# A PEER layer's first expert product: each expert column split in two pieces instead of three

## The chip, the cores and the metric

The kernel runs on one core of one Trainium2 chip. The metric is device time in microseconds of one execution, the median of several. Before the change it is 2997.09 us, the median of three runs that lay between 2996.09 and 2999.84 us. One further execution was taken with the hardware profiler; all rows below are from it.

## The reference

Two transformer blocks follow each other over 256 tokens of width 2048. The change lies in the last part of the second, a layer that chooses 16 experts for each of 8 heads out of 16384 and works on the rows that belong to them:

```python
def peer(xn, peer_w_q, peer_sub_keys, peer_u, peer_v):
    ...
    qh = (xt @ peer_w_q).reshape(T, PEER_HEADS, 2, PEER_HALF)
    sub = jnp.einsum("thpc,hpnc->thpn", qh, peer_sub_keys).astype(jnp.float32)
    v1, i1 = lax.top_k(sub[:, :, 0], PEER_TOPK)
    v2, i2 = lax.top_k(sub[:, :, 1], PEER_TOPK)
    ...
    experts = e1 * N_KEYS + e2
    gates = jax.nn.softmax(vals, axis=-1).astype(xn.dtype)
    def chunk_fn(args):
        xc, ec, gc = args
        u_sel = jnp.take(peer_u, ec, axis=0)
        h = jnp.einsum("cd,chkd->chk", xc, u_sel)
        a = jax.nn.gelu(h, approximate=False) * gc
        v_sel = jnp.take(peer_v, ec, axis=0)
        return jnp.einsum("chk,chkd->cd", a, v_sel)
```

`u` and `v` hold 16384 rows of 2048 numbers. The first expert product is `h`, the second the last line.

## The kernel before

The kernel is one long program. After the first block and the second block's convolution and attention comes the query product (`w_pq`), then the first expert product, then a choosing stage (lines 1169 to 1279), then the second expert product (lines 1315 to 1337).

The first expert product is computed in two ways at once. Of each row of `u`, the first 1408 numbers go through TensorE for **all** 16384 experts. The experts are ordered in 128 columns `e2` of 128 experts each, and one column is a block of 128 partitions by 1408 numbers, 11 chunks of 128. The other 640 numbers are fetched only for the chosen experts: GpSimd gathers 128 rows at a time with an indirect DMA (line 1026, 320 KB each, two per column, 256 in all), and VectorE multiplies each by the tokens and sums it (line 1040, a "dot" in what follows).

A column is handled in pieces (`UPC`), three of them before: 512, 512 and 384 numbers wide. For each piece SyncE issues a load into a raw buffer (line 421 or 424), ScalarE rounds it to `hi` (line 427), VectorE forms the remainder `lo` (line 428), and TensorE then does three matmuls for each chunk of 128 (`three`, lines 461, 464 and 465): `hi` with the tokens' high part, `hi` with their low part, `lo` with their high part. So the first two matmuls of a piece need `hi`, and the third needs `lo`. A column has 33 matmuls of 256 columns of tokens, the stage 4224.

The buffers are rings. `hi` and `lo` each have `UB[1]` buffers. Raw buffers come from two places (`u_raw`): `UB[0]` buffers of a pool, named `ur` in the trace, and `XRAW` slices of a block of the output array `ha` that isn't written yet, named `ha`. Before, that is 6 and 8 raw buffers. From column 92 on, the output array's block is about to be written, and pieces use the pool's buffers alone:

```python
        k = nraw[0] % (UB[0] + XRAW)
        if e2 >= (EB - 2) * EC - 4:
            k = 0
        nraw[0] += 1
        return None if k < UB[0] else xraws[k - UB[0]][:, :n]
```

A load into a raw buffer waits until the piece that was in it has both been rounded and had its remainder formed, which is the end of its line 428. The slices of `ha` lie where the query product's buffers and the first gathered rows (`kq`) lay, so they can be loaded only when the dots over `kq` are done.

Gathered rows have a ring of their own, 4 buffers and 6 more in the last block of `ha`. At column 106 (lines 1144 to 1146) all pending dots are done and the ring shrinks to 4. From column 1 on a gather waits for the last matmul of the column before it.

Each engine works its instructions off in one fixed order. That order is set when the program is built, by a scheduler that moves instructions among the stages, so pieces of the first columns are loaded and split while the query product still runs. A small generator, `step`, lets the steps of the heads' top-16 choice run on VectorE between the pieces until about column 100.

Of the kernel before, what the change touches and what calls it, by code (L numbers as in the profile page):

```python
# [30 lines left out]
NSUB = 1  # L31
STEPS = ((0, 0), (1, 0))
SEV = 5
UPC = ((0, 4), (4, 4), (8, 3))
EC = 16
EB = P // EC
XRAW, XROW = 8, 6
TK = (2, 4, 6)
EG = (0, 0, 0, 2, 4, 6, 8, 8)
TKU = (2, 12, 22, 32, 42)  # L40
UL = 126
UB = (6, 4)
VPACE, UPACE, UR = False, True, 4
N32 = (6, 7)
VR, VB, VLAG = 6, 3, 2
# [156 lines left out]
def body(ctx: ExitStack, tc: tile.TileContext, a, out):  # L202
# [214 lines left out]
    def wsplit(src, pool, n, nm, bufs, sb, size=None, raw=None):  # L417
        if first:
            raw = first.pop(0)
        elif raw is not None:  # L420
            nc.sync.dma_start(raw, src)
        else:
            raw = pool.tile([P, size or n], F32, tag="raw", name=nm + "r", bufs=bufs)[:, :n]
            nc.sync.dma_start(raw, src)
        hi = pool.tile([P, size or n], F32R, tag="hi", name=nm + "h", bufs=sb)[:, :n]
        lo = pool.tile([P, size or n], F32R, tag="lo", name=nm + "l", bufs=sb)[:, :n]
        S.activation(hi, raw, AF.Copy)  # L427
        low.append(V.tensor_tensor(lo, raw, hi.bitcast(F32), OP.subtract))  # L428
        return hi, lo
# [617 lines left out]
    def step():  # L1047
        while running:
            if next(running[0], True) is None:
                return True  # L1050
            running.pop(0)
# [53 lines left out]
    def block(b):  # L1105
        return ha[:, b].rearrange("p t b -> p (t b)")

    urows[0].more = [block(EB - 1)[:, k * (D - DU):(k + 1) * (D - DU)] for k in range(XROW)]
    xraws = [block(EB - 2)[:, k * UPC[0][1] * P:(k + 1) * UPC[0][1] * P] for k in range(XRAW)]
    nraw = [0]  # L1110

    def u_raw(e2, n):
# [7 lines that stand above are left out]
# [10 lines left out]
    for i in range(64):  # L1130
        ps = banks.one("ps_u")
        for b in range(2):
            e2 = 2 * i + b
            for p, (c0, n) in enumerate(UPC):
                if (b, p) in STEPS or (i % SEV == 0 and (b, p) == (1, 1)):
                    step()
                hi, lo = wsplit(a["u_dense"][e2][:, c0 * P:(c0 + n) * P], us, n * P, "u", *UB, UPC[0][1] * P,
                                u_raw(e2, n * P))
# [224 lines left out]
```

## Time and profile before

| | |
|---|---|
| median of three runs | 2997.09 us (2996.09 to 2999.84) |
| the profiled execution's own time | 2991.99 us |
| its span, first to last instruction | 2990.2 us |
| TensorE (PE) busy | 2923.6 us, 98% |
| VectorE (DVE) busy | 2395.6 us, 80% |
| ScalarE (ACT) busy | 1567.1 us, 52% |
| GpSimd (POOL) busy | 881.0 us, 29% |
| first expert product | from 1794.3 to about 2316.7 us of the span |

The profiled execution is 5.1 us under the median; 1.8 us of it lie outside the span. PE is TensorE's matmuls and PEld its weight loads. Matmuls overlap, so their durations add up to more than the time; what a matmul costs is read from how many start in a stretch. SPq is the queue of SyncE, which issues the loads.

### The profile page before, as it was taken

The numbers are of one execution on the slowest core, as the hardware profiler recorded it, in microseconds if no ns is written. First come the engines' busy times: TensorE is split into PE (matmuls) and PEld (weight loads), VectorE is DVE, ScalarE is ACT, GpSimd is POOL, SyncE is SP. The second block draws the span as 40 slices with busy tenths as digits, with TensorE's granted clock in tenths as the row PEclk, the third lists the DMA queues.
The fourth block names the chain that finished last, engine by engine and source line by source line (L and its number), as shares of the span: only waits on it lengthen the run. The fifth ranks groups of instructions, "written<-read, shape, count | busy, mean of one in ns | idle before, by whom it ended". The sixth has DMA issues, their size and how long they took to land. (4 is left out here: it accounts for less than half of the span.)

```text
span 2990.2 us, 49998 instructions
## 1 busy us (share of the span) xinstructions
PE 2923.6 (98%) x18472; PEld 2616.6 (88%) x18472; DVE 2395.6 (80%) x4392; ACT 1567.1 (52%) x2312; POOL 881.0 (29%) x670
## 2 busy tenths in 40 slices
PE   8999999999999999998999989999999999999999
PEld 7888888888888888888978989999999988888887
DVE  6567666777777776768998787999987988999998
ACT  5564555555545454546565534555555554444444
POOL 0000000000000000000000055666654897777786
PEclk9999999999999999999999999999999999999999
DMA  6545666656565666554534679999989348999998
GB/s 223 155 141 186 190 188 187 189 185 189 189 189 186 190 189 190 186 167 147 157 106 136 223 246 335 334 334 337 313 302 322 114 139 319 333 338 342 328 339 317
DMA packets 211143, 686.35 MB, mean 230 GB/s; under 512 B 29265, under 2 KB 47057, under 8 KB 210513
## 3 DMA queue, kind: packets, MB, share of 16 engines
q1 hardware_dynamic: 169776, 523.15, 53.4%
q0 software_dynamic: 41120, 160.01, 15.5%
q8 instruction: 144, 2.36, 0.3%
q14 instruction: 103, 0.84, 0.1%
HBM read 677.41 MB, written 5.64 MB: 228 GB/s over the span
## 5 line engine op out<-in xcount | busy, mean ns | idle before, releaser
L428 DVE TENSOR_TENSOR wl<-wr,wh 128x1024 fp32r<-128x1024 f32 x572 | 699.6, 1224 | 357.5 <-ACT wh L427 356.9
L427 ACT ACTIVATE wh<-wr 128x1024 fp32r<-128x1024 f32 x572 | 605.4, 1059 | 672.5 <-PE ps_dn L448 118.0
L976 POOL TENSOR_TENSOR tk_c<-tk_v 128x256 f32<-128x256 f32 x16 | 11.2, 702 | 1709.2 <-DVE tk_v L968 1708.9
L1026 POOL DMA_INDIRECT vrows<-in_v_rows,ex x256 | 393.8, 1538 | 119.3 <-DVE yg L1302 59.1
L465 PE MATMUL ps_u<-u_a,ul 128*128 128x256 f32 x1408 | 399.8, 284 | 9.7 <-DVE ul L428 9.5
L461 PE MATMUL ps_u<-u_a,uh 128*128 128x256 f32 x1408 | 397.9, 283 | 1.0 <-ACT uh L427 1.0
L464 PE MATMUL ps_u<-u_a,uh 128*128 128x256 f32 x1408 | 397.4, 282 | 0.0
L448 PE MATMUL ps_w_up<-u_a,wh 128*128 128x512 f32 x968 | 342.9, 393 | 0.0
L1318 ACT ACTIVATE vhi<-vraw 128x1472 fp32r<-128x1472 f32 x128 | 184.0, 1437 | 263.5 <-PE y L1335 260.9
L1334 PE MATMUL y<-vlo,ah 128*128 128x512 f32 (+1 forms) x768 | 297.8, 388 | 1.2 <-DVE vlo L1321 1.2
L1333 PE MATMUL y<-vhi,ah 128*128 128x512 f32 (+1 forms) x768 | 295.1, 384 | 3.5 <-ACT ah L1325 3.5
L1335 PE MATMUL y<-vhi,al 128*128 128x512 f32 (+1 forms) x768 | 296.5, 386 | 0.1
L465 PEld LDWEIGHTS ps_u<-u_a,ul 128*128 128x128 f32 x1408 | 266.4, 189 | 13.6 <-DVE ul L428 13.4
L450 PE MATMUL ps_w_up<-u_a,wl 128*128 128x256 f32 x968 | 270.4, 279 | 0.0
L461 PEld LDWEIGHTS ps_u<-u_a,uh 128*128 128x128 f32 x1408 | 266.5, 189 | 1.3 <-ACT uh L427 1.3
L464 PEld LDWEIGHTS ps_u<-u_a,uh 128*128 128x128 f32 x1408 | 266.4, 189 | 0.0
L448 PE MATMUL ps_dn<-ff,wh 128*128 128x512 f32 x704 | 248.7, 396 | 4.9 <-DVE ff L289 3.4
L1321 DVE TENSOR_TENSOR vlo<-vraw,vhi 128x1472 fp32r<-128x1472 f32 x128 | 216.1, 1688 | 40.1 <-ACT vhi L1318 40.0
L448 PEld LDWEIGHTS ps_w_up<-u_a,wh 128*128 128x128 f32 x968 | 181.4, 187 | 43.5
L1302 DVE SCALAR_TENSOR_TENSOR yg<-vrows,av,yg 128x576 f32<-128x576 f32 x256 | 208.6, 815 | 7.9 <-DMA vrows<-in_v_rows,ex 3.6
L427 ACT ACTIVATE uh<-ur 128x512 fp32r<-128x512 f32 (+1 forms) x228 | 135.6, 597 | 136.2 <-PE ps_u L464 97.7
L450 PE MATMUL ps_dn<-ff,wl 128*128 128x256 f32 x704 | 199.3, 283 | 3.8 <-DVE wl L428 3.8
(399 smaller groups left out, 7442.5 us busy)
## 6 DMA issues: line engine op xcount, KB each, us to landing
vraw<-in_v_dense SPq DMA_DIRECT2D x128, 736.0 KB, 7.2
wr<-in_w_up SPq DMA_DIRECT2D x176, 512.0 KB, 3.5
wr<-in_w_dn SPq DMA_DIRECT2D x88, 512.0 KB, 3.6
ur<-in_u_dense SPq DMA_DIRECT2D x152, 256.0 KB, 5.1
ha<-in_u_dense SPq DMA_DIRECT2D x104, 256.0 KB, 5.2
wr<-in_w_in SPq DMA_DIRECT2D x44, 512.0 KB, 3.5
wr<-in_w_cv SPq DMA_DIRECT2D x32, 512.0 KB, 3.6
wr<-in_w_ga SPq DMA_DIRECT2D x32, 512.0 KB, 3.5
```

Source lines behind the costliest of these rows:

```text
L427: S.activation(hi, raw, AF.Copy)
L428: low.append(V.tensor_tensor(lo, raw, hi.bitcast(F32), OP.subtract))
L448: PE.matmul(ps[:, j], hi[:, s], x[:, c0 + k, 0:2 * T], start=first and k == 0, stop=False, skip_group_check=True)
L450: PE.matmul(ps[:, j, T:], lo[:, s], x[:, c0 + k, 0:T], start=False, stop=last and k == KC - 1, skip_group_check=True)
L461: m = PE.matmul(o, wh, xh, start=start, stop=False, skip_group_check=True)
L464: PE.matmul(o, wh, xl, start=False, stop=False, skip_group_check=True)
L465: return PE.matmul(o, wl, xh, start=False, stop=stop, skip_group_check=True)
L1026: g = G.indirect_dma_start(out=v, out_offset=None, in_=a[name], in_offset=bass.IndirectOffsetOnAxis(ap=ex[:, tt, s:s + 1], axis=0))
L1321: vlo.append(V.tensor_tensor(lo, raw, hi.bitcast(F32), OP.subtract))
L1333: PE.matmul(o, st, hi[:, c:c + n], start=e2 == 0, stop=False, skip_group_check=True)
L1334: PE.matmul(o, st, lo[:, c:c + n], start=False, stop=False, skip_group_check=True)
L1335: mm = PE.matmul(o, sl, hi[:, c:c + n], start=False, stop=e2 == P - 1, skip_group_check=True)
```

## The change

Three tables of numbers change. A column is cut in two pieces of 768 and 640 numbers. The `hi` and `lo` rings have three buffers of 768 numbers each instead of four of 512. The raw ring has three pool buffers and five slices of `ha`, of 768 numbers, instead of six and eight of 512. For column 92 and after, that leaves three raw buffers.

```diff
-UPC = ((0, 4), (4, 4), (8, 3))
+UPC = ((0, 6), (6, 5))
 EC = 16
 EB = P // EC
-XRAW, XROW = 8, 6
+XRAW, XROW = 5, 6
...
-UB = (6, 4)
+UB = (3, 3)
```

TensorE's matmuls stay in the same order. The following places show what moves on the other engines; `x2` at the end of a row means twice in a row.

SyncE, from the last loads of the query product (`wr`) to the first loads into `ha`; `subd` and `sub` are scores that go out to memory and come back. Before:

```order
L424 DMA ur<-in_u_dense 128x512
L424 DMA ur<-in_u_dense 128x384
L424 DMA wr<-in_w_pq 128x1024 x4
L1080 DMA subd<-sub 128x512
L424 DMA wr<-in_w_pq 128x1024
L1080 DMA subd<-sub 128x512 x2
L421 DMA ha<-in_u_dense 128x512 x2
L421 DMA ha<-in_u_dense 128x384
```

Now:

```order
L424 DMA ur<-in_u_dense 128x768
L424 DMA wr<-in_w_pq 128x1024 x4
L1080 DMA subd<-sub 128x512
L424 DMA wr<-in_w_pq 128x1024
L1080 DMA subd<-sub 128x512 x2
L421 DMA ha<-in_u_dense 128x640
L421 DMA ha<-in_u_dense 128x768
```

The first piece that needs a slice of `ha` was the seventh, the first of column 2; it is now the fourth, the second of column 1.

VectorE, where the query product ends and the expert product begins; `kq,hg` are dots, `ul<-ur,uh` and `ul<-ha,uh` the remainders of pieces. Before:

```order
L1040 ISA kq,hg<-kq,xg 128x640
L1040 ISA hg 128x1
L428 TENSOR_TENSOR ul<-ur,uh 128x512
L428 TENSOR_TENSOR ul<-ur,uh 128x384
L428 TENSOR_TENSOR ul<-ha,uh 128x512 x2
```

Now:

```order
L1040 ISA kq,hg<-kq,xg 128x640
L1040 ISA hg 128x1
L428 TENSOR_TENSOR ul<-ha,uh 128x640
L428 TENSOR_TENSOR ul<-ha,uh 128x768
L428 TENSOR_TENSOR ul<-ha,uh 128x640
```

Before, the fifth and sixth pieces' remainders (the last two pieces of column 1) stand behind the last of the dots over `kq`. Now the remainders of all three pieces that have pool buffers stand earlier, among the query product's, and the first one behind the dots is that of a piece in `ha`.

VectorE late in the stage, where only the pool's buffers are used, one column's work. Before:

```order
L428 TENSOR_TENSOR ul<-ur,uh 128x512 x2
L428 TENSOR_TENSOR ul<-ur,uh 128x384
L1040 ISA urows,hg<-urows,xg 128x640
L1040 ISA hg 128x1
L1040 ISA urows,hg<-urows,xg 128x640
```

Now:

```order
L428 TENSOR_TENSOR ul<-ur,uh 128x768
L428 TENSOR_TENSOR ul<-ur,uh 128x640
L1040 ISA urows,hg<-urows,xg 128x640
L1040 ISA hg 128x1
L1040 ISA urows,hg<-urows,xg 128x640
```

The dots keep their place behind a column's pieces; a column has one remainder less.

## Rows read from the trace of the kernel before

**Rows 1.** The page's first part and its line of TensorE's granted clock.

```profile
PE 2923.6 (98%) x18472; PEld 2616.6 (88%) x18472; DVE 2395.6 (80%) x4392; ACT 1567.1 (52%) x2312; POOL 881.0 (29%) x670
...
PEclk9999999999999999999999999999999999999999
```

**Rows 2.** Busy time in stretches of the first expert product; the first row names the columns.

```profile
core 0: us, PE busy (x) PEld busy (x) DVE busy (x) ACT busy (x) POOL busy (x), PEclk, DMA share, GB/s
...
2000.00:2100.00 100.00, 99.59 (x835) 98.99 (x834) 95.80 (x250) 56.39 (x93) 63.39 (x51) 1.00 0.97 338
...
2245.30:2308.80 63.50, 63.14 (x531) 62.78 (x529) 50.29 (x105) 34.96 (x56) 32.94 (x28) 1.00 0.96 337
```

**Rows 3.** Waits of TensorE, 1815 to 2220 us: in total, times, longest, us.

```profile
PE ps_u L465 <- DVE ul L428: 2.8, 7, 0.5
```

**Rows 4.** Waits from 2165 to 2317 us, all engines.

```profile
ACT uh L427 <- DMA ur<-in_u_dense: 17.2, 15, 1.9
...
PE ps_u L465 <- DVE ul L428: 3.9, 6, 2.2
```

**Rows 5.** Waits of SyncE's queue, 2165 to 2317 us.

```profile
SPq L424 <- DVE ul L428: 85.3, 71, 6.6
```

**Rows 6.** A piece's load, rounding and remainder, timelines of SyncE, ScalarE and VectorE.

```profile
2256.36 0.33 SPq L424 DMA_DIRECT2D ur<-in_u_dense  x1
...
2262.43 0.63 ACT L427 ACTIVATE uh<-ur 128x512 fp32r<-128x512 f32 x1 [1.92 <-DMA ur<-in_u_dense]
...
2264.16 0.82 DVE L1040 CUSTOM_DVE_ANT_0 urows<-urows,xg 128x640 f32<-128x640 f32 x1 [1.88 <-DMA urows<-in_u_rows,ex]
2264.91 0.08 DVE L1040 DVE_READ_ACCUMULATOR2_ANT hg<- 128x1 f32 x1
2264.91 1.76 DVE L428 TENSOR_TENSOR ul<-ur,uh 128x512 fp32r<-128x512 f32 x3
```

**Rows 7.** Landing times of pieces issued from 2250 to 2317 us.

```profile
DMA to landing us min/median/max: 3.5/5.1/6.3
```

**Rows 8.** Landing times of the two pieces issued at 2238.5 and 2238.9 us.

```profile
DMA to landing us min/median/max: 2.5/2.5/2.5
```

**Rows 9.** Landing times of gathered rows issued from 2250 to 2317 us.

```profile
DMA to landing us min/median/max: 4.7/5.8/7.0
```

**Rows 10.** Groups by shape, 2250 to 2317 us: count, busy us, mean ns, idle before.

```profile
L428 DVE TENSOR_TENSOR ul<-ur,uh 128x512 fp32r<-128x512 f32 x32 | 21.1, 686 | 4.4 <-ACT uh L427 3.4 <-PE ps_u L465 0.7
L427 ACT ACTIVATE uh<-ur 128x512 fp32r<-128x512 f32 x32 | 20.3, 634 | 19.2 <-PE ps_u L464 8.1 <-DMA ur<-in_u_dense 7.9 <-DVE ul L428 3.2
...
L428 DVE TENSOR_TENSOR ul<-ur,uh 128x384 fp32r<-128x384 f32 x16 | 8.8, 553 | 1.6 <-ACT uh L427 1.4
L427 ACT ACTIVATE uh<-ur 128x384 fp32r<-128x384 f32 x16 | 8.4, 525 | 8.9 <-PE ps_u L464 8.8
```

**Rows 11.** TensorE's matmuls of the product in the stage's first 6.75 us.

```profile
1794.30:1801.05 6.75, 5.79 (x47) 5.67 (x47) 0.00 (x0) 1.00 0.79 226
```

**Rows 12.** The stage's beginning, timelines of TensorE, VectorE, SyncE and ScalarE.

```profile
1804.43 0.58 PE L465 MATMUL ps_u<-u_a,ul 128*128 128x256 f32 x1 [3.18 <-DVE ul L428]
...
1803.69 1.15 DVE L428 TENSOR_TENSOR ul<-ur,uh 128x512 fp32r<-128x512 f32 x2
...
1803.90 4.66 SPq L421 DMA_DIRECT2D ha<-in_u_dense x8
...
1808.70 0.63 ACT L427 ACTIVATE uh<-ha 128x512 fp32r<-128x512 f32 x1 [9.73 <-DMA ha<-in_u_dense]
...
1810.11 0.39 PE L465 MATMUL ps_u<-u_a,ul 128*128 128x256 f32 x1 [0.23 <-DVE ul L428]
```

**Rows 13.** Two-microsecond stretches at the beginning, columns as in rows 2.

```profile
1806.00:1808.00 2.00, 2.00 (x12) 2.00 (x11) 0.00 (x0) 0.00 (x0) 0.00 (x0) 0.57 0.90 299
```

**Rows 14.** VectorE at column 106, first and last of nine dots, and what follows.

```profile
2223.84 0.82 DVE L1040 CUSTOM_DVE_ANT_0 urows<-urows,xg 128x640 f32<-128x640 f32 x1
...
2229.81 0.82 DVE L1040 CUSTOM_DVE_ANT_0 urows<-urows,xg 128x640 f32<-128x640 f32 x1
...
2230.55 1.75 DVE L428 TENSOR_TENSOR ul<-ur,uh 128x512 fp32r<-128x512 f32 x3
```

**Rows 15.** Stretches behind column 106, columns as in rows 2.

```profile
2232.00:2236.00 4.00, 4.00 (x27) 4.00 (x27) 0.91 (x2) 1.15 (x2) 1.42 (x2) 0.70 0.84 284
2236.00:2240.00 4.00, 3.53 (x30) 3.32 (x29) 2.62 (x5) 2.17 (x4) 1.12 (x1) 1.00 0.59 203
2240.00:2244.00 4.00, 3.74 (x31) 3.54 (x30) 4.00 (x12) 1.67 (x3) 2.65 (x3) 1.00 0.84 241
```

## Prediction

> **What bounds the kernel now.** I read the page's first part, then the stage's busy time by stretches, then who waits for whom, then single timelines. TensorE is busy 98% of the span at a granted clock that reads full in every slice [rows 1], so time is won or lost only where TensorE waits. Inside the stage it hardly does: from 1815 to 2220 us it waited 2.8 us in all, each time for a piece's remainder on VectorE [rows 3], and from 2165 to the end 3.9 us [rows 4]. Its pace undisturbed is 531 matmuls in 63.50 us [rows 2], 0.1196 us each; a column of 33 takes 3.95 us. The reader should see how thin the cover over this is. VectorE is busy 95.8 of 100 us in the middle and 50.3 of 63.5 us near the end, and the DMA engines run at a share of 0.96 to 0.97 in both [rows 2]. In the last part, where only the pool's raw buffers are used, SyncE's queue waits for remainders 71 times, 85.3 us in all [rows 5], and ScalarE waits 15 times for a load [rows 4]. A ring in which the load waits for the buffer and the next engine waits for the load is already turning there at nearly the rate TensorE needs.
>
> **The change part by part.**
>
> *Fewer, larger splits.* From 686 and 553 ns for 512 and 384 numbers [rows 10] a remainder costs about 1.04 ns a number on top of a fixed part, so 768 and 640 take 952 and 819 ns; a column's remainders fall from 1.925 to 1.771 us, 0.15 us less, 20 us of VectorE over 128 columns. Roundings by the same rows take 852 and 743 ns. TensorE hides all of that: it waits for remainders 2.8 us in 405 [rows 3], which is the most that faster splits can return there. Against it stands that `hi` and `lo` of a piece now may be begun two pieces ahead of TensorE (11 chunks, 3.95 us) and take 1.7 us, where it was three pieces (11 to 12 chunks) and 1.3 us, so 0.4 us of lead is lost beside dots that block VectorE for 0.8 us each [rows 14]. I take 0 for columns 2 to 91, with bounds of -2.8 (all waits gone) and +5 (they grow almost threefold).
>
> The Trainium skill, Perfetto Trace Analysis, section Optimizing Scalar/DVE Operations, says that larger operations improve throughput if the engine is saturated, and that where Scalar or Vector aren't saturated but cause bubbles on other engines, breaking instructions up lets work finish sooner. By its first half the middle of the stage would gain, by its second the end would lose; the 95.8% and 79% agree with a reading in both directions.
>
> *The start.* Before, TensorE did 47 matmuls [rows 11], then stood 3.18 us, because the fifth piece's remainder is behind the dots over `kq`; it then ran the 66 matmuls of six pieces out and took the seventh piece's third matmul, the first that needs its remainder, at 1810.11 [rows 12]. Now three pieces, 17 chunks or 51 matmuls, are all split early, so it stops 4 matmuls later, near 1801.6. The fourth piece is in `ha`, whose first load was issued at 1803.90 and reached ScalarE at 1808.70 [rows 12]. With a quarter more bytes (0.15 us), a rounding of 0.74 and a remainder of 0.82 us, its third matmul starts at about 1810.5, 0.4 us later than the 1810.11 and with 15 matmuls fewer done: 0.4 + 15 x 0.1196 = 2.2 us lost. Behind its wait TensorE ran at a clock of 0.57 [rows 13], the lower level, for 14 or so matmuls; I expect that spell once again, so no difference. Bounds: 0.5 (the dots come sooner) and 5 (two slow spells).
>
> *The ring of three.* From column 92 on a load waits for the piece three before it, not six. One turn is: release to issue 0.05, landing, landing to rounding 0.11, rounding 0.80 (mean of 852 and 743), 0.03, then the remainder's place in VectorE's queue, and the remainder 0.885 (mean of 952 and 819). A turn of the old ring [rows 6]: issued 2256.36, rounded from 2262.43, the remainder held until 2264.91 by a dot that itself waited for its row. Without landing and queue that is 1.87 us. For the queue I take 0.5 us, a third of the 1.5 us that two dots in the way hold it, at 0.75 us from dot to dot [rows 14]. Three pieces give TensorE 16.5 chunks, 49.5 matmuls, 5.92 us of work. So the turn fits if landing takes up to 3.55 us.
>
> Landing is what the trace doesn't show for this ring. Under load the smaller pieces take 5.1 us at the median [rows 7]. Two pieces of 256 and 192 KB issued when VectorE had just held everything up took 2.5 us [rows 8], and gathered rows of 320 KB, the size of the new smaller piece, take 5.8 us [rows 9]. So the ends are 2.5 and 5.8 us. With at most three own pieces in flight the queue in front is shorter, but the gathers stay and each piece has half as many bytes again; I take 4.4 us, nearer to rows 7. Then a turn is 4.4 + 1.87 + 0.5 = 6.77 us against 5.92, 0.85 us lost each. Pieces 187 to 255 make 23 turns: 19.6 us. The first turn starts with some 0.9 us of lead, so **18.7 us**. At 2.5 us nothing is lost (turn 4.87 us); at 5.8 us a turn is 8.17 us, 23 x 2.25 = 52 us.
>
> The waits would be short, one of some 0.3 us before each piece. Two such waits behind column 106 left the granted clock at 1.00 (second and third row of [rows 15]), so I add nothing for the clock.
>
> The Trainium skill, DMA: Bandwidth & Descriptors, section Anatomy of one DMA — SWDGE (gpsimd) path, fits a DMA's time as 2.0 us plus bytes over 436 GB/s. For 384 and 320 KB that is 2.9 and 2.75 us, an estimate by that page; the turn would be 5.2 us and nothing would be lost, which speaks against my sum. The page's fit (2.5 to 2.6 us for 192 to 256 KB) agrees with the 2.5 us of the idle moment and not with the 5.1 us under load.
>
> *The drain at column 106.* Nine dots in a row, 2223.84 to 2230.55, hold back the remainders [rows 14], and TensorE lost a wait of 2.2 us [rows 4] and a slow spell at 0.70 [rows 15]. With a starved ring there is less lead before it, but the three loads land meanwhile. I take +1, bounds -2 and +4.
>
> Sum: 0 + 2.2 + 18.7 + 1 = 21.9, so 22 us; the profiled execution's 2991.99 us would become 3014. The median of the runs is 5.1 us above that execution, so **3019 us**.
>
> **The rivals.**
>
> *The ring of three keeps up* (same). Condition: landing at or below 3.55 us, because fewer bytes are queued. For it: rows 8. Against it: DMA share 0.96 [rows 2] and the two gathers per column, whose amount doesn't change. Left are 2.2 us at the start and 1 at the drain: 3000 us.
>
> *VectorE's relief shows* (faster). Place: the whole stage. With one remainder less a column and landing below 3.55 us, waits of 2.8 and 3.9 us go [rows 3, 4], and with the drain's wait its slow spell (27 matmuls in 4 us where 33.4 fit [rows 15], 0.8 us); if the start also costs nothing, 2997 - 7.5 = 2989.5 us. It decides only if both the landing and the start go well. Against it: the lead that is lost.
>
> *Landing as slow as the gathers'* (much slower). For it: same size, same engines, 5.8 us at the median [rows 9]. Against it: a starved ring asks for less. 52 + 3 = 55: 3052 us.
>
> **How the numbers follow.** Forecast 0.65, keeping up 0.12, relief 0.09, slow landing 0.14. The forecast's own range is 3009 to 3031 us: landings of 4.0 and 4.9 us give turns of 6.37 and 7.27 us, 9.5 and 30 us with the lead taken off, and 3 us beside. A measurement here can tell about 0.2%, 6 us, from no change. Forecast and slow landing lie above 3003 us, together 0.79; keeping up lies within, a little of it beyond: same 0.12; faster 0.09. The range takes in the upper edge of keeping up and most of the way to slow landing, 2998 to 3044.
>
> **What the changed profile would show.** Right: from column 92 on SyncE's waits for remainders stay, ScalarE's waits for `ur` grow from 17.2 us and 15 times to dozens of waits, TensorE waits for roundings and remainders some 20 us between column 92 and the end, the clock stays at 1.00 there, and loads land in 4.0 to 4.9 us. At the start one wait of about 8 us in place of 3.18 and 0.96. From column 3 to 91 nothing changes. Wrong: landing at 3.5 us or less, or TensorE's waits spread over the columns before 92, or a clock of about 0.5 between the short waits, which would cost far more.

## The result and the profile after

The changed kernel takes 3014.84 us, the median of four runs (3011.78 to 3018.78), against 2996.59 us for the kernel before on the same chip (four runs, 2995.85 to 2999.84). The ratio is 1.0063, 95% interval 1.0050 to 1.0077: slower, by 15 to 23 us. The forecast was 3019 us, 22 us more than before. The profiled execution took 3015.2 us with a span of 3013.4 us, 23.2 us longer than the span before. The profiled execution of before lay 4.6 us under the median of these runs and this one lies 0.4 us above its own, so 5 of the 23 us are a matter of which execution was profiled.

Where the 23.2 us lie is read off TensorE's timeline, by the start of the first matmul of a column (the last number of a row is what the stretch that ends there grew by):

| us of the span | before | after | grew by |
|---|---|---|---|
| query product begins | 1680.23 | 1681.31 | 1.1 |
| column 0 begins | 1794.37 | 1798.56 | 3.1 |
| column 3 begins | 1814.29 | 1819.12 | 0.6 |
| column 92 begins | 2167.63 | 2173.67 | 1.2 |
| column 104 begins | 2215.78 | 2226.72 | 4.9 |
| column 108 begins | 2236.22 | 2249.69 | 2.5 |
| last matmul of column 127 begins | 2316.51 | 2338.36 | 8.4 |
| end | 2990.22 | 3013.41 | 1.3 |

So 15.8 us of the growth are in columns 92 to 127 (the tail in what follows), where only the pool's three raw buffers serve, and 3.8 us in the query product and the first three columns together. The query product and the first columns belong together, since the first load into `ha` is issued when the gathered rows over `kq` are done, whatever TensorE has reached: 123.7 us behind the query product's begin before, 123.3 us now.

The busy time by stretches, columns as in [rows 2], for columns 92 to 127 of the kernel before and then of the changed one:

```profile
2167.63:2316.51 148.88, 145.03 (x1195) 143.42 (x1194) 124.78 (x276) 78.59 (x130) 76.35 (x63) 0.99 0.91 311
```

```profile
2000.00:2100.00 100.00, 99.19 (x829) 98.78 (x828) 95.29 (x224) 52.71 (x67) 64.09 (x53) 1.00 0.95 333
...
2173.67:2338.36 164.69, 152.75 (x1195) 146.72 (x1194) 121.52 (x240) 73.69 (x95) 74.79 (x64) 0.98 0.85 286
```

The same 1195 instructions of TensorE (36 columns of 33 matmuls and seven others) take 148.9 us in one and 164.7 us in the other. VectorE, ScalarE and the DMA engines do less per microsecond, not more: nothing got saturated; rather, the engines wait for each other in a circle. In the middle (first row of after) nothing has changed against [rows 2].

The waits in columns 92 to 127 of the changed kernel (in total, times, longest, us), with [rows 4, 5] as their counterpart:

```profile
ACT uh L427 <- DMA ur<-in_u_dense: 75.1, 50, 6.5
DVE ul L428 <- ACT uh L427: 39.4, 37, 4.1
...
PEld ps_u L465 <- DVE ul L428: 13.5, 24, 2.1
PE ps_u L465 <- DVE ul L428: 8.0, 17, 1.8
...
PE ps_u L461 <- ACT uh L427: 3.4, 4, 1.6
```

```profile
SPq L424 <- DVE ul L428: 104.0, 66, 5.7
```

ScalarE's waits for a load went from 15 (17.2 us) to 50 (75.1 us), for 69 pieces. From there the wait is passed on: VectorE waits for the rounding, TensorE for either. The last line is SyncE's queue, which still waits for remainders before it issues a load, as it did before [rows 5]. TensorE's waits are 11.4 us here and not the 22.5 us that it takes beyond its undisturbed 142.2 us (36 columns of 3.95 us): the view counts a wait from the modelled end of the matmul before it, and leaves out what a lower clock costs. One piece of that ring, in the timelines of ScalarE, VectorE and TensorE (start, duration, instruction, idle time before it and its releaser):

```profile
2289.76 0.85 ACT L427 ACTIVATE uh<-ur 128x768 fp32r<-128x768 f32 x1 [1.19 <-DMA ur<-in_u_dense]
2295.22 0.74 ACT L427 ACTIVATE uh<-ur 128x640 fp32r<-128x640 f32 x1 [4.61 <-DMA ur<-in_u_dense]
...
2295.99 0.82 DVE L428 TENSOR_TENSOR ul<-ur,uh 128x640 fp32r<-128x640 f32 x1 [4.15 <-ACT uh L427]
...
2296.01 0.39 PE L461 MATMUL ps_u<-u_a,uh 128*128 128x256 f32 x1 [1.59 <-ACT uh L427]
2296.23 0.28 PE L464 MATMUL ps_u<-u_a,uh 128*128 128x256 f32 x1
2296.87 0.39 PE L465 MATMUL ps_u<-u_a,ul 128*128 128x256 f32 x1 [0.36 <-DVE ul L428]
```

All three engines stand until the load of this piece lands at 2295.11; it was issued at 2288.31, when the piece three before it had its remainder. It is one of the slowest: it and the two behind it took 6.8, 7.8 and 7.5 us to land. Landing times of the pieces in this stretch, which before were [rows 7]:

```profile
DMA to landing us min/median/max: 2.8/4.5/7.8
```

Two stretches of the changed kernel behind its longest waits show TensorE at a lower granted clock (the seventh number, behind the five engines' busy times; 0.50 is the lower of its two levels, and 0.64 a mean over both):

```profile
2246.00:2249.00 3.00, 3.00 (x16) 3.00 (x15) 0.18 (x1) 0.00 (x0) 0.13 (x1) 0.50 0.84 296
...
2296.00:2300.00 4.00, 3.63 (x17) 3.43 (x18) 3.25 (x6) 2.34 (x3) 1.29 (x1) 0.64 0.57 189
```

The first answers to the spell that the kernel before also had behind its drain [rows 15]. The second is new and had not been forecast: 18 matmuls started 0.21 us apart in place of 0.12, 1.7 us.

### The profile page after: what moved, and what is told of

It is laid out like the page before. It is cut to its first block, busy times and chain, and to the rows that moved or that the text cites. A ratio compares the mean times of both kernels' runs of the same rounds, so it can differ in the third digit from the quotient of the medians.

```text
span 3013.4 us, 49238 instructions
## 1 busy us (share of the span) xinstructions
PE 2935.5 (97%) x18472; PEld 2625.6 (87%) x18472; DVE 2391.7 (79%) x4264; ACT 1551.9 (51%) x2184; POOL 872.0 (29%) x670
## 4 chain that ended last, share of the span: by engine, by line
PE 75%; DVE 7%; POOL 6%; issue 5%; DMA 4%; ACT 2%; DVEq 0%; POOLq 0%; ACTq 0%; SPq 0%
PE ps_w_up L448 11%; PE ps_w_up L450 6%; PE ps_dn L448 5%; POOL vrows L1026 5%; PE ps_u L465 4%; PE ps_u L464 4%; PE ps_u L461 4%; PE ps_dn L450 3%; PE y L1335 2%; PE y L1334 2%; PE y L1333 2%; DMA ur<-in_u_dense 2%; PE ps_w_ga L448 2%; PE ps_w_cv L448 2%; PE ps_w_gb L448 2%
## 5 line engine op out<-in xcount | busy, mean ns | idle before, releaser
L1026 POOL DMA_INDIRECT vrows<-in_v_rows,ex x256 | 385.4, 1505 | 130.2 <-DVE yg L1302 70.0
L465 PEld LDWEIGHTS ps_u<-u_a,ul 128*128 128x128 f32 x1408 | 268.5, 191 | 17.8 <-DVE ul L428 17.6
L427 ACT ACTIVATE uh<-ur 128x768 fp32r<-128x768 f32 (+1 forms) x141 | 112.9, 802 | 167.7 <-DMA ur<-in_u_dense 77.1
```

What stands on the lines that cost most here:

```text
L465: return PE.matmul(o, wl, xh, start=False, stop=stop, skip_group_check=True)
L1026: g = G.indirect_dma_start(out=v, out_offset=None, in_=a[name], in_offset=bass.IndirectOffsetOnAxis(ap=ex[:, tt, s:s + 1], axis=0))
```

## The experiments

The theory was the prediction's: from column 92 a piece's load waits for the piece three before it, and issue, landing, rounding and remainder (the turn) take longer than TensorE needs for three pieces. The rivals are the larger pieces themselves, or the shorter `hi` and `lo` rings, or VectorE's dots, or something of the last part (the drain, the block written there).

**One raw buffer more.** `four_raw` keeps the two pieces and gives the pool four raw buffers, two of each size:

```diff
-UB = (3, 3)
+UB = (4, 3)
...
-raw = pool.tile([P, size or n], F32, tag="raw", name=nm + "r", bufs=bufs)[:, :n]
+raw = (pool.tile([P, n], F32, tag="raw%d" % n, name=nm + "r", bufs=2) if nm == "u" else
+       pool.tile([P, size or n], F32, tag="raw", name=nm + "r", bufs=bufs)[:, :n])
```

> The changed kernel with four pool raw buffers instead of three (two of 768 and two of 640 numbers, which fit; the hi and lo rings stay at three of 768). Theory A, the ring of loads: a turn (issue, landing, rounding, remainder; 6.9 us in the changed kernel's last part) now has four pieces of TensorE work, 7.9 us, so it fits; columns 92 to 127 take 148 to 151 us instead of 164.7, and the time falls to 2998 to 3003 us. Rival B, the larger pieces and the hi and lo ring of three: both are unchanged, so the time stays at 3011 to 3018 us and the last part at 160 us or more.

Ratio to before 1.0024 (1.0014 to 1.0034), 3001.73 us. Columns 92 to 127 of this kernel, columns of the row as above:

```profile
2173.91:2325.09 151.18, 145.44 (x1195) 143.50 (x1194) 122.37 (x240) 73.32 (x95) 74.55 (x64) 0.99 0.89 306
```

151.2 us against 164.7 with three and 148.9 before: one more buffer returns 13.5 of the 15.8 us, with the piece size, the dots and the shorter `hi` and `lo` rings left as they were. (The tail is 0.2 us over the expected range.) The time in front of column 3 did not come back: here SyncE issues the pool's first loads only from 1799.5 us on, behind the scores that it sends to memory, where the changed kernel issues the first at 1703.8; why they stand there in its order isn't shown.

**The old pieces in a short ring.** `thirds4` and `thirds5` are the kernel before with `UB = (4, 4)` and `UB = (5, 4)` in place of `(6, 4)`.

> The kernel before, with its pieces of 512, 512 and 384 numbers and four hi and lo buffers, but four pool raw buffers instead of six. Theory A: a turn is about 4.4 us landing plus 1.45 us of own work plus 0.4 us of queue, 6.3 us, against four pieces or 5.3 us of TensorE work; 26 turns lose 1.0 us each, less the 6 us that this part had lost anyway: 3012 to 3025 us, and ScalarE waits for loads in most pieces after column 92. Rival B: pieces are small and the hi and lo ring has four, so nothing is lost: 2995 to 3000 us.

> The kernel before with five pool buffers in the raw ring from column 92 on. By the ring's sum five pieces of 4,4,3 chunks give TensorE 18.3 chunks, 6.6 us of work, and a turn with landing 4.8, 1.57 us of its own work (roundings and remainders of 512 and 384 numbers) and 0.5 us of queue is 6.9 us: 0.3 us short per turn of five pieces, 22 turns, 6 us. So columns 92 to 127 take 150 to 157 us, ratio 1.000 to 1.003, between the kernel before (six, 148.9) and four (171.9). Rival, a threshold in bytes in flight or in the number of loads rather than a turn: five behaves as four, over 162 us and over 1.005.

`thirds4` took 3020.51 us, 1.0080 (1.0064 to 1.0097), `thirds5` 3001.50 us, 1.0025 (1.0016 to 1.0035). Columns 92 to 127 of the first, then of the second:

```profile
2173.83:2345.72 171.89, 154.92 (x1195) 146.86 (x1194) 123.89 (x276) 79.80 (x130) 72.02 (x63) 0.98 0.84 270
```

```profile
2170.30:2326.21 155.91, 148.00 (x1195) 145.06 (x1194) 124.62 (x276) 78.59 (x130) 72.14 (x63) 0.98 0.88 299
```

With unchanged piece sizes the tail takes 148.9, 155.9 and 171.9 us for six, five and four buffers: the loss comes with the ring's length and not with the size of a piece. Five buffers lie between six and four, as a turn has it; a threshold would have put them with four. The turn's parts, as means over the pieces behind column 92 (from the timelines; the turn also holds the 0.03 to 0.04 us from release to issue; "need" is the matmuls of a ring's pieces times TensorE's 0.1196 us; `no_dots` and `no_gather` follow below):

| us | landing | to rounding | rounding | queue on VectorE | remainder | turn | need |
|---|---|---|---|---|---|---|---|
| before, six | 5.09 | 0.81 | 0.60 | 1.08 | 0.65 | 8.28 | 7.89 |
| `thirds5` | 4.91 | 0.27 | 0.60 | 0.83 | 0.65 | 7.28 | 6.58 |
| `thirds4` | 4.39 | 0.16 | 0.59 | 0.62 | 0.65 | 6.45 | 5.26 |
| after, three larger | 4.62 | 0.15 | 0.79 | 0.47 | 0.89 | 6.94 | 5.92 |
| `four_raw` | 5.17 | 0.56 | 0.79 | 1.03 | 0.89 | 8.48 | 7.89 |
| `no_dots` | 4.69 | 0.33 | 0.79 | 0.07 | 0.89 | 6.81 | 5.92 |
| `no_gather` | 3.32 | 0.54 | 0.79 | 0.64 | 0.89 | 6.20 | 5.92 |

A measured turn is the pace of the whole ring, so what it has above the need is the loss itself and no reason for it: "to rounding" and "queue" hold waiting that others cause. Landing, rounding and remainder alone hold none. Their sum lies above the need in the three kernels with the slowest tails (6.30 us of 5.92 after, 5.63 of 5.26 in `thirds4`, 6.37 of 5.92 in `no_dots`) and under it in the others (6.34 of 7.89 before, 6.85 of 7.89 in `four_raw`, 5.00 of 5.92 in `no_gather`). `thirds5` is the nearest, 6.16 of 6.58: the 0.4 us that are left don't cover its queue of 0.83 us.

**No gathers.** `no_gather` is the changed kernel without gathers from column 92 on (`late[0]`); the dots stay and work on rows left in their buffers.

```diff
+    late = [False]
...
+            if late[0]:
+                ring = urows[0].v + urows[0].more
+                pend.append((ring[urows[0].i % len(ring)], tt, s))
+                urows[0].i += 1
+                continue
             pend.append((urows[0].get("u_rows", tt, s, pace), tt, s))
...
+            late[0] = e2 >= 92
```

> The changed kernel without the row gathers from column 92 on; the dots stay and work on rows that are there already (the gathered part of h is not computed for the last slots). Theory A with landing set by the load of the DMA engines: loads land in 2.5 to 3.3 us instead of 4.6, a turn is about 5.2 us against 5.92, and the last part takes 146 to 151 us: 2997 to 3002 us. If landing doesn't depend on the gathers it stays near 4.5 us and so does the loss: 3010 us or more. Rival C, VectorE's queue: the dots are as many as before, so the loss stays at 10 us or more.

2997.98 us, 1.0011 (1.0001 to 1.0020). Its columns 92 to 127, and its pieces' landing times:

```profile
2179.05:2327.75 148.70, 144.88 (x1195) 143.54 (x1194) 121.61 (x239) 74.69 (x95) 4.08 (x3) 0.99 0.62 182
```

```profile
DMA to landing us min/median/max: 2.7/3.3/5.0
```

With the same ring of three, the tail is back at 148.7 us. VectorE's queue did not get shorter (0.64 us against 0.47), so it isn't the dots' waits for rows that went. So the disputed term of the turn is the landing, 4.6 us beside the gathers and 3.3 us without them, and the condition of the rival "keeps up" (3.55 us or less) was the right line to draw.

**No dots.** `no_dots` keeps the gathers and leaves out the dots from column 92 on (`late[0]` as in `no_gather`; `hg` is set to zero at the start).

```diff
             v, tt, s = pend.pop(0)
+            if late[0]:
+                continue
...
```

> The changed kernel with the gathers, but without the dots from column 92 on, the nine at column 106 included (hg is set to zero at the start, the gathered part of h is not computed for the last slots). Theory A: landing stays at 4.4 to 4.7 us and only the queue on VectorE goes, so a turn is about 6.5 us and 23 turns lose 13 us; the stop at column 106 goes too; the last part takes 154 to 158 us: 3004 to 3009 us. Rival C, VectorE's queue: the loss goes, 2996 to 3000 us.

3011.71 us, 1.0056 (1.0039 to 1.0073), against 1.0063 for the changed kernel. Its tail:

```profile
2172.82:2334.25 161.43, 150.43 (x1196) 144.95 (x1194) 71.50 (x100) 72.92 (x95) 70.74 (x64) 0.99 0.86 291
```

That is a miss on size: VectorE lost 50 us of work in the tail (busy 71.5 us, from 121.5) and only 3.3 us came back. That is hardly more than the tail's own spread: `warm` and `warm46` below, with the changed kernel's tail, have 168.4 and 163.4 us. The table shows why it is so little: the queue fell by 0.40 us, but landing and the step behind it grew by 0.25, so most of what the queue returns is waited for elsewhere in the circle. By place, columns 104 to 107, where the row of dots had stood, took 18.0 us instead of 23.0, and the columns behind them 2.1 us more.

**The `hi` and `lo` rings alone.** `thirds_hl3` is the kernel before with `UB = (6, 3)`.

> The kernel before with three hi and lo buffers instead of four, the raw ring left at six: the other half of what the change made smaller, alone. Theory (the raw ring alone costs): columns 92 to 127 take 148 to 152 us, the time is within 0.1% of before, 0.999 to 1.0015. Rival (the hi and lo ring of three shares the loss): columns 92 to 127 take over 155 us, ratio over 1.002, or columns 3 to 91 over 356 us.

3001.42 us, 1.0025 (1.0015 to 1.0035): the theory's "within 0.1%" was wrong, and a sign of the rival came true (columns 3 to 91 over 356 us), though the tail took 150.5 us as the theory had it. Columns 3 to 91 of the kernel before, then of this one:

```profile
1814.29:2167.63 353.34, 351.08 (x2939) 349.14 (x2938) 334.45 (x856) 197.46 (x327) 223.30 (x179) 1.00 0.96 333
```

```profile
1815.83:2174.50 358.67, 353.73 (x2940) 350.25 (x2939) 337.25 (x855) 201.30 (x327) 203.97 (x178) 1.00 0.96 328
```

and TensorE's waits there, which the kernel before has for 2.8 us over about the same columns [rows 3]:

```profile
PE ps_u L465 <- DVE ul L428: 4.8, 11, 0.9
```

Three buffers of 512 give TensorE 11 chunks, against 14.7 in four and 16.5 in the changed kernel's three of 768. So this ring has its own price, 5.3 us, in the part where VectorE is fullest; the changed kernel, with larger buffers, takes 1.2 us more than before there.

**The ring from column 56.** `ring56` is the changed kernel with the pool's raw buffers alone from column 56 (`e2 >= (EB - 2) * EC - 40` in place of `- 4`).

> The changed kernel with the pool's three raw buffers alone in use from column 56 on and not from 92. It tells whether what the last part costs is the ring's turn or something of the last part (the row of dots at column 106, the drained block). Theory: every turn of three pieces takes landing 4.6 + 1.87 + a queue of 0.5 to 1.0 us (VectorE is fuller in the middle), so 7.0 to 7.5 us against 5.92, and the 24 turns of columns 56 to 91 lose 25 to 37 us more: ratio to before 1.0145 to 1.019. Rival: the loss belongs to the last part, columns 3 to 91 stay within 5 us of 354.5, ratio under 1.008.

3037.45 us, 1.0137 (1.0120 to 1.0154). Columns 56 to 91 of the changed kernel, then of this one:

```profile
2029.93:2173.67 143.74, 142.65 (x1191) 142.03 (x1189) 136.17 (x309) 76.11 (x98) 90.93 (x73) 1.00 0.92 324
```

```profile
2032.69:2195.35 162.66, 150.35 (x1191) 143.33 (x1189) 134.14 (x306) 74.05 (x97) 84.24 (x72) 1.00 0.88 292
```

18.9 us more in 36 columns without a drain and without an output block: the loss goes with the ring and not with the place. It is smaller than was expected (25 to 37 us); VectorE's queue was 0.43 us there and not 0.5 to 1.0. Against TensorE's undisturbed 142.2 us the 24 turns lose 20.4 us, 0.85 us each.

**The clock at the start.** `warm` and `warm46` are the changed kernel with 60 and 46 matmuls that nobody reads, placed between the third and the fourth piece, so that TensorE does not stand there.

```diff
+                if (e2, p) == (1, 1):
+                    pt = ptp.tile([P, 512], F32, tag="tp", name="ps_fill")
+                    for _ in range(60):
+                        fill = PE.matmul(pt[:, :T], xa[:, 0, 0:P], xa[:, 1, 0:T], start=True, stop=True,
...
+                        after(fill, mm, False)
...
```

> The changed kernel, with 60 matmuls that nobody reads placed on TensorE between the third and the fourth piece, where it stood waiting for the first piece in the output array's block. Theory: the start cost 3.8 us and not 2.2 because the matmuls behind that wait ran at the lower clock (0.21 us each between 1811.7 and 1814.4) with the loads already landed, where the kernel before had the same spell hidden under a further wait for loads. Then the matmuls of the fourth piece start 0.12 us apart, the first three columns take 19 us instead of 20.6, the span falls by 1.3 to 2 us, and the tail stays at 164 to 165 us: ratio to before 1.0055 to 1.0065. Rival: the spell is not from the wait, or the loads bound the first columns anyway: the first three columns stay at 20.6 us within 0.3.

> As in warm, but with 46 matmuls that nobody reads in place of 60. The 60 kept the granted clock at full but ended 1.6 us after the fourth piece's remainder was ready, so they put a wait of their own in place of the spell. Theory: with 46 the fourth piece's third matmul starts within 0.2 us of its remainder's end, the clock stays at full from there, the first three columns take 18.3 to 18.9 us instead of the 20.6 us of the changed kernel, query product and first columns together 135.5 to 136.5 instead of 137.8. The tail is unchanged (164 to 169 us). Rival: the loads behind the fourth piece bound the start, and the first three columns take 19.8 us or more.

`warm` took 3014.43 us, 1.0079 (1.0065 to 1.0093). The fourth piece in the changed kernel, on TensorE's timeline, then stretches of the start in the changed kernel and in `warm`:

```profile
1810.85 0.58 PE L461 MATMUL ps_u<-u_a,uh 128*128 128x256 f32 x1 [4.87 <-ACT uh L427]
...
1811.71 0.58 PE L465 MATMUL ps_u<-u_a,ul 128*128 128x256 f32 x1
```

```profile
1810.00:1814.00 4.00, 3.09 (x12) 2.80 (x13) 2.08 (x3) 2.32 (x3) 0.00 (x0) 0.50 1.02 383
1814.00:1816.00 2.00, 2.00 (x11) 2.00 (x11) 0.47 (x1) 0.97 (x2) 0.29 (x1) 0.53 0.97 302
```

```profile
1810.80:1814.00 3.20, 3.20 (x30) 3.20 (x29) 1.78 (x3) 2.11 (x4) 0.41 (x1) 1.00 0.92 329
```

The granted clock is 0.50 behind a wait of 4.87 us, and 1.00 where TensorE kept working before it. The kernel before had its slow spell in front of a further wait, for the rounding of a piece whose load was still on its way [rows 12], so matmuls at full speed would only have waited longer there:

```profile
1809.38 0.38 PE L461 MATMUL ps_u<-u_a,uh 128*128 128x256 f32 x1 [0.96 <-ACT uh L427]
```

From the fourth piece's third matmul to column 3 the changed kernel takes 7.41 us (1811.71 to 1819.12) and `warm` 5.46 (1811.03 to 1816.49): 1.95 us for the same 46 matmuls, which is what the lower clock costs. The filling itself ended 1.6 us too late, so the first columns fell only from 20.6 to 20.1 us and not to the expected 19, and the ring's own spread (tail 168.4 us here, not 164 to 165) covered it in the total.

`warm46` was meant to take that wait away and did not settle it: 3014.97 us, 1.0068 (1.0052 to 1.0084). In its profiled execution the first load into `ha` was issued 9.3 us behind column 0's begin instead of 6.1 and took 5.75 us to its rounding, the filling ran out at about 1809.4 us, TensorE stood 3 us and the clock fell after all:

```profile
1812.00:1814.00 2.00, 1.36 (x4) 1.07 (x5) 0.83 (x1) 1.25 (x2) 0.00 (x0) 0.50 0.83 329
```

The first columns took 24.5 us. That is the rival's number (19.8 us or more), but not its reason alone, since the lower clock was still there. How much the start could return is open. Over the seven profiles of two-piece kernels that begin alike or nearly so, query product and first three columns take 137.5 to 140.9 us together; the three kernels with six pool buffers of 512 take 133.4 to 134.1 us. `thirds5` and `thirds4`, with the old pieces and five and four pool buffers, take 136.6 and 138.0 us, so the start seems to cost more with fewer buffers, whatever the size of a piece.

**Spreading the drain.** `spread` is the kernel before with its nine dots at column 106 done gradually:

```diff
+            if 96 <= e2 < (EB - 1) * EC - 6:
+                u_dot(max(3, 8 - (e2 - 96) // 2))
             if e2 == (EB - 1) * EC - 6:
                 u_dot(0)
```

> The kernel before, with the pending dots done a little at a time from column 96 on (the backlog allowed falls by one every two columns, from 8 to 3), so that no row of nine dots stands at column 106. It tests how much of column 92 to 127 the kernel before lost to that row: 148.9 us there against 142.2 us for 36 columns of 3.95 us. If the row of dots costs it (theory), columns 104 to 127 fall from 100.7 us to 95 to 97 us, columns 92 to 103 stay within 0.8 us of 48.2, and the time is 0.9975 to 0.9990 of before, some 4 to 6 us less in the profile. Rival: the smaller backlog makes VectorE wait for gathered rows, and the loss only spreads out: columns 92 to 127 stay at 148 us or more, ratio 0.9995 to 1.003.

2995.39 us, 1.0003 (0.9994 to 1.0012): no difference, as the rival had it. Columns 92 to 127 of this kernel, then columns 104 to 107:

```profile
2170.09:2317.41 147.32, 143.62 (x1195) 142.09 (x1194) 124.42 (x276) 78.91 (x130) 77.88 (x63) 1.00 0.92 314
2218.92:2236.52 17.60, 16.72 (x140) 16.34 (x138) 15.08 (x35) 9.34 (x16) 8.05 (x7) 1.00 0.82 276
```

Columns 104 to 107 fell from 20.4 to 17.6 us and columns 92 to 127 to 147.3, 1.6 us less and not the expected 4 to 6. What this kernel still loses in its tail, 5.1 us, is spread over it. No kernel tried beats the one before.

## Why the prediction was right

The sign, the place and the mechanism were those forecast, and the time lay 4 us under the forecast, inside its narrower range (3009 to 3031 us). The sum, 22 against the 23.2 us by which the profiled execution grew, is better than its terms: two were mis-sized, and that they cancel is luck. The 4 us come from another step: the forecast took the median to lie 5.1 us above the profiled execution, as before, and this time both lay together (3014.84 and 3015.2 us).

- *The ring of three.* The turn was put at 4.4 + 1.87 + 0.5 = 6.77 us. Measured are 4.62 for landing, 1.86 for rounding, remainder and the steps between, 0.47 for the queue, 6.94 together, the drain's pieces among them. `ring56`, where no drain is, gives the forecast's 0.85 us a turn. What was mis-sized is the amount **against before**: 23 turns were priced against TensorE's undisturbed 5.92 us, as if the kernel before ran this part undisturbed. It did not: it took 148.9 us for 142.2 us of work, a loss that its own rows showed in part [rows 4, 15]. The changed kernel loses 22.5 us there, and 15.8 of them are new; 18.7 and 1 for the drain had been forecast. (The three profiles with this tail have 163.4 to 168.4 us, so 14.5 to 19.5 us are new by them.)
- *The drain.* Columns 104 to 107 grew by 2.5 us; 2.7 turns at 0.85 us would be 2.3 of it. How much is the drain's isn't shown: without the dots these columns took 5.0 us less in the changed kernel (`no_dots`), and with the dots spread 2.8 us less in the kernel before (`spread`), but in both the columns behind them took longer. The +1 is within what these leave open.
- *The clock.* "I add nothing for the clock" was wrong by one spell, 18 matmuls and 1.7 us, at 2296 to 2300 us. The waits were not the even 0.3 us before each piece that it was argued from: TensorE's view has 21 of them for 69 pieces, the longest 1.8 us. Most kept the clock, as argued; it fell behind the one shown above (1.6 and 0.4 us in one piece).
- *The start.* The fourth piece's third matmul came at 1811.71, or 1810.6 when the 1.1 us by which the query product began later are taken off: 1810.5 had been forecast. The step that failed is "I expect that spell once again, so no difference". Before, the slow spell [rows 13] ran while the next loads were still on their way, and the wait of 0.96 us behind it took it up. Now the next two loads landed at 1811.78 and 1812.80, during the spell but before TensorE came to them, and it showed: 1.95 us by `warm`. (Some 0.2 us less by an estimate: at full speed the fifth piece's third matmul would have come at 1813.5, and its remainder ended at 1813.70.) So 3.8 and not 2.2 us, within the bounds of 0.5 to 5; but in three other profiles with the same start (`no_gather`, `no_dots`, `ring56`) it is 6.5 to 6.8 us more than before, beyond them: the wait there is 7.4 to 9.3 us and 22 to 25 matmuls behind it run slowly, where the profile of the changed kernel has 4.87 us and 18.
- *Columns 3 to 91.* 1.2 us against 0; `no_dots` and `warm`, with the same code there, have 0.6 and 0.5. VectorE's relief returned nothing that shows; the waits that it could have taken away were 2.8 us [rows 3]. `thirds_hl3` shows that the other side of that argument, lead lost in the `hi` and `lo` rings, is a real cost with buffers of 512.
- *Not in the sum.* The query product ran 3.1 us longer. That the larger pieces between its own on VectorE and ScalarE did it isn't shown: it takes 115.3 to 117.4 us in the profiles of two-piece kernels that begin alike, and 113.5 to 116.1 us in those of three-piece ones. The wait that follows took it up: 4.87 us at the fourth piece, where about 8 had been forecast for a column 0 that begins as before. Another 2.4 us lie in front of the query product and behind column 127, where nothing was changed.

Of the signs named beforehand, SyncE's waits, ScalarE's dozens of waits, the landing (4.5 us) and the quiet columns 3 to 91 came as said. Three did not: TensorE's waits by the view (11.4 us, not some 20), the clock (two spells, not 1.00 throughout) and the wait at the start.

Of the rivals, "keeps up" fell on its condition: the pieces landed in 4.5 us at the median, and 3.3 us only with the gathers gone. "As slow as the gathers'" fell the other way. "VectorE's relief" needed both the short landing and a start that costs nothing, and had neither.

The fit of the Trainium skill, DMA: Bandwidth & Descriptors, section Anatomy of one DMA — SWDGE (gpsimd) path, 2.0 us plus bytes over 436 GB/s, gives 2.75 to 2.9 us for these pieces, an estimate by that page, which states it for transfers that GpSimd issues, while SyncE issues these. It agrees with the shortest landing, 2.8 us, and with no typical one here. The Trainium skill, Perfetto Trace Analysis, section Optimizing Scalar/DVE Operations, says that where Scalar or Vector aren't saturated but cause bubbles on other engines, breaking instructions up may let work finish sooner. No run here shows that: `thirds4`, smaller pieces in a ring that holds 14.7 chunks for 16.5, is slower still than the changed kernel (171.9 against 164.7 us in the tail), but its ring differs along with its pieces.

## What to carry to other kernels

Where a load waits for its buffer, compare one full turn (issue, landing under this load, every engine that must finish before the buffer is free, with its queue) with the time in which the consumer uses up all the buffers' contents. Fewer and larger buffers are slower as soon as the turn is the longer one. Take the turn from its parts that hold no waiting: the turn as measured in a running ring is only its pace. Price the change against what the kernel before really takes in that stretch, not against the engine's undisturbed pace. And look at what a slow-clock spell runs beside: here it cost nothing that shows in front of a wait that ended later (before), and up to 1.95 us where the data was ready in time (after, by `warm`).

## What was not expected of the hardware

Landing time follows what else is under way. Pieces of 320 and 384 KB land in 3.3 us at the median at 182 GB/s, without gathers, and in 4.5 us at 286 GB/s with them; smaller pieces of 192 and 256 KB took 4.39 us on average in a ring of four and 5.09 us in a ring of six. The larger pieces took 5.17 us in a ring of four and 4.62 us in one of three. So shortening a ring gives part of its loss back through faster landing, and speeding up another part of the turn gives part of its gain away again: without the dots the queue fell by 0.40 us and the turn by 0.13.
